# adaLN weight tiles spread over the four column groups of the tensor array, and put behind the score products of a head

## The chip, the cores and the metric

One Trainium2 chip, one core of it. The metric is the device time of one execution in microseconds (us), lower is better. Median before: 1648.79 us.

## What is computed

A two-layer hybrid backbone on 512 latent tokens behind 256 context tokens, 1024 channels, all in f32 accuracy. The part that the change touches is the adaLN modulation: for each layer, the two condition vectors (latent and context) go through silu and a product with a weight of 1024 x 3072, which gives shift, scale and gate.

```python
def layer(x, ctx, c, c_ctx, l):                       # core of the reference
    shift, scale, gate = split(silu(c) @ ada_w[l] + ada_b[l], 3)
    h = rms(x, norm_g[l]) * (1 + scale) + shift       # the same for ctx with c_ctx
    x = x + gate * mixer[l](h_ctx, h)                 # l = 0: HGRN2, 16 heads; l = 1: RG-LRU
```

## The kernel before, in words

**Staging.** All weights come from memory as tiles of 128 x 1024 f32 (512 KB) in one planned order (class Weights, DMA issue at L114 on SyncE's queue). A tile of the mixers is split by ScalarE (L129) and VectorE (L130) into two float32r parts, and each of their products is three matmuls (mm3, L308 to L310). Tiles of the adaLN weights (48: two layers, six blocks each, four tiles a block) are used as they come, in f32.

**An adaLN block** (ada_block, L223 to L249) makes 512 of the 3072 columns. The stationary operand is `sc`, silu of the two condition vectors padded to 32 columns, in eight chunks of 128 channels. It fills only 32 of the array's 128 columns, so the four tiles of a block go to four column groups (tile_position (0, 32j)), each with a part of the contraction:

```python
        for j in range(4):
            w = wget("ada", l, b, j)
            for k in range(2):
                PE.matmul(ps[32 * j:32 * j + 32, :], lhsT=sc[:, 2 * j + k, :], rhs=w[:, 512 * k:512 * k + 512],
                          start=k == 0, stop=k == 1, tile_position=(0, 32 * j))
            if j < 3:
                yield 480.0
```

So tile j is two matmuls of 512 columns, both in group j. An f32 matmul stands in the trace as two records (passes). Then ScalarE copies the block out of PSUM (blk, L233), four small matmuls add the four groups and turn the result (adat, L237), and VectorE adds the bias (L242, L246). Each yield ends a step: four steps with a tile, one with the transposes.

**Where the steps stand.** TensorE takes its work in program order. Blocks (0,0) to (0,3) are made in the start, in an order written by hand (START): a step "a0" is the next step of block (0,0), "r" the norm of the input (msh L259, rbh L269), "h3" chunk 3 of the modulated input, "f21" the part of the first head's product 2 with chunk 1. The blocks (0,4), (0,5) and (1,0) to (1,5) are made within heads 0, 1 and 9 to 14, one block a head. A head is a generator (hgrn): the diagonal scores (dg, L436), seven levels of scores (lv, L456), the states, the outputs. Scores of 32 keys use four column groups too: 24 matmuls of 32 columns. Between the steps of a head, interleave puts the products into the next head (in, L308 to L310), which are the filler. weave puts one step of the adaLN block after every third step of that filler.

Of the kernel before, what the change touches and what calls it, by code (L numbers as in the profile page):

```python
# [13 lines left out]
P = 128  # L14
CTX = 256
LAT = 512
NT = CTX + LAT          # tokens, context first
HN = NT // 2            # token half
ROWS, GW = 8, 64        # latent grid
DK = 8                  # 128-channel chunks of the model width  # L20
NH = 16                 # HGRN2 heads
NC = NT // P            # chunks of 128 tokens
NLEV = 7                # block sizes 1, 2, ... 64 within a chunk
NM = 5                  # of these, the ones within 32 tokens
RH = 8                  # RG-LRU heads
EPS = 1e-6

# the order of the start: a step of adaLN block b (ab), the norm (r), chunk k of h (hk), the weights of the first head's
# product y (wy), their part with chunk k of h (fky), the split of the first value weights (v)
# [3 lines left out]
# columns of the packed parameters  # L33
# [7 lines left out]
# columns of the constants: identity, row selector, 1/1024, 1/128  # L41
# [10 lines left out]
def perm(ap):  # L52
    """latent columns in column-major grid order, walked row by row"""
    return ap.rearrange("p (w r) -> p r w", r=ROWS)
# [6 lines left out]
def phase(main, weight, filler, total):  # L61
    """interleave up to the next None of main, if weight is that of one phase"""
    interleave(upto(main, weight), weight, filler, total)
# [12 lines left out]
class Nothing:  # L76
    """stands in for the program while the order of the weight tiles is taken down"""
# [16 lines left out]
class Weights:  # L94
    """the stream of [128, 1024] weight tiles, loaded ahead and split into two float32r parts"""
# [60 lines left out]
def interleave(main, weight, filler, total):  # L156
    """after each step of main (yields give its weight), its share of the filler (yields give its size)"""
    done, n = 0.0, 0.0
    for w in main:
        n += w  # L160
        while filler is not None and done < total * min(1.0, n / weight):
            try:
                done += next(filler)
            except StopIteration:
                filler = None
    run_all(filler)


def build(tc, ins, out, plan):
# [19 lines left out]
    # ---- constants, small parameters, the residual stream  # L189
# [24 lines left out]
    # silu of both condition vectors, padded to 32 columns  # L214
# [7 lines left out]
    # ---- adaLN: six blocks of 512 columns, four parts of the contraction side by side in the array  # L222
    def ada_block(l, b):  # L223
        ps = atile(f"ada{l}_{b}")
        for j in range(4):
            w = wget("ada", l, b, j)
            for k in range(2):
                PE.matmul(ps[32 * j:32 * j + 32, :], lhsT=sc[:, 2 * j + k, :], rhs=w[:, 512 * k:512 * k + 512],  # L228
                          start=k == 0, stop=k == 1, tile_position=(0, 32 * j))
            if j < 3:  # L230
                yield 480.0
# [19 lines left out]
    # ---- h = rms(x) * g * (1 + scale) + shift, as two float32r parts  # L251
    def rstd_of(accs, ones, tag, parts, between=()):
        """1 / sqrt(mean + eps) of each token from its squares (chunks of 128 tokens; the mean is over the partitions
        and accs), on all partitions: PSUM tiles of so many chunks"""
# [23 lines left out]
    def sumsq(accs, groups, tile_, k, c):  # L278
        """the squares of chunk k of the channels, summed by groups of chunks; the first of three groups on GpSimd"""
# [13 lines left out]
    def hchunk(l, k, i, rs, scr):  # L293
        """chunk k of h for one stretch of tokens; layer 0 keeps the latents in row-major order"""
# [9 lines left out]
    def mm3(ps, pairs, first=True, last=True, skip=False):  # L304
        """exact products of split operands: ps += sum over (whi, wlo, xhi, xlo) of whi xhi + whi xlo + wlo xhi"""
# [9 lines left out]
    # ================= layer 0  # L315
# [98 lines left out]
    def prep(h):  # L414
        """operands of the first two score steps"""
# [9 lines left out]
    def hgrn(h):  # L425
# [4 lines left out]
        # scores [key, query]: same token (both directions), then pairs of neighbouring blocks of 1, 2, ... 64 tokens;  # L430
        # up to 32 tokens the array works on four groups of 32 keys at once
# [9 lines left out]
        for l in range(NLEV):  # L441
# [5 lines left out]
            for c in range(NC):  # L447
                for g in range(P // w):
# [5 lines left out]
                    else:  # L454
                        rhs = QQ[:, 0, o - w:o]
                    PE.matmul(ps[w * g:w * g + w, w * c:w * c + w], lhsT=kt[:, o:o + w], rhs=rhs, start=c == 0,  # L456
                              stop=c == NC - 1, skip_group_check=True, tile_position=(0, w * g))
            kv = view(KK, 0, [[2 * B, n], [NT + B, 2], [1, B]])
# [22 lines left out]
        # keys with tokens on the partitions (in place), for the chunk states  # L481
# [7 lines left out]
        # states that enter the chunks, in the order of each direction  # L489
# [19 lines left out]
        # outputs, head norm, gate; latents written in column-major order of the grid  # L509
# [71 lines left out]
    # ---- start: norm of layer 0, the first head's q and forget gates as the chunks of h come  # L581
# [4 lines left out]
    # lower bound of layer 0: the first row of the softmax over the rows  # L586
# [44 lines left out]
    # layer 1: 8 softplus(-lam) = 8 (max(-lam, 0) + log1p(exp(-|lam|))), log1p as 2 atanh(y / (2 + y))  # L631
# [24 lines left out]
    # ---- heads: the products into the next head fill the tensor engine between the steps of this one  # L656
    def weave(gen, gens, every):
        """a step of gens after each so many of gen"""
        side = chain_(gens)
        for i, x in enumerate(gen):  # L660
            yield x
            if i % every == 0:
                next(side, None)
        run_all(side)

    def chain_(gens):
        for g in gens:
            yield from g
# [18 lines left out]
    for h in range(NH):  # L687
        if h == 0:
            fill, total = [v_item(0), in_item(0, 3), weave(head_in(1), extra(1), 3)], 54700.0
        elif h < NH - 1:  # L690
            fill, total = [weave(head_in(h + 1), extra(h + 1), 3)], 45300.0 if h < NH - 2 else 23500.0
        else:
            fill, total = [in_item(h, 3), out_item((h - 3, h - 2, h - 1))], 31400.0
        interleave(hgrn(h), HW, chain_(fill), total)
# [10 lines left out]
    # ================= layer 1: the context first  # L705
# [23 lines left out]
    def after(*names):  # L729
        """queue ScalarE's instructions behind the last ones of these kinds"""  # L730
# [14 lines left out]
    def conv(j, e, i, ps):  # L745
        """the centred convolution of one stretch of tokens; then the two parts of the result"""
# [39 lines left out]
    def mixer(j, groups):  # L786
        """gates of both directions, decay a, driven input u, scans; groups of directions and output chunks are taken in
        turn. ScalarE goes through its table sets once a group: sigmoid, exp and tanh, sqrt"""
# [4 lines left out]
        for keys in groups:  # L793
# [19 lines left out]
            # with T = tanh(-log(a)): 1 - a^2 = T (1 + a^2)  # L813
# [64 lines left out]
    # ---- the last head out, its first half ahead of the second; final norm  # L878
# [52 lines left out]
# ---- host: layouts only  # L931
def _layout(inp):
# [4 lines left out]
    chan = lambda v: v.reshape(-1, P).T                      # [n*128] -> [128, n]  # L937
    x = a["x"][0].reshape(ROWS, GW, 1024).transpose(1, 0, 2).reshape(LAT, 1024)
    xs = np.concatenate([a["ctx"][0], x], 0)                 # tokens x channels
# [24 lines left out]
    # adaLN columns: shift and scale chunks side by side, then the gates  # L964
# [4 lines left out]
    w = np.stack(blocks, 1)                                  # l, b, k, p, 512  # L969
    o["ada"] = w.reshape(2, 6, 4, 2, P, 512).transpose(0, 1, 2, 4, 3, 5).reshape(2, 6, 4, P, 1024)  # L970
# [31 lines left out]
```

## Time and profile before

| | |
|---|---|
| median of 3 runs | 1648.79 us (1645.66 to 1650.98) |
| span of the profiled execution | 1643.9 us |
| time of the profiled execution outside its span | not listed; the median is 4.9 us above the span |
| TensorE busy | 1595.2 us, 97% of the span |
| VectorE, ScalarE, GpSimd busy | 73%, 52%, 1% |
| mean DMA rate | 71 GB/s |
| adaLN products (L228) | 192 records, 81.2 us busy, 4% of the chain that ended last |

The chain that ended last is followed back from the last instruction. A busy TensorE counts as busy also when only one of its column groups works.

### The profile page before, as it was taken

The numbers are of one execution on the slowest core, as the hardware profiler recorded it, in microseconds if no ns is written. First come the engines' busy times: TensorE is split into PE (matmuls) and PEld (weight loads), VectorE is DVE, ScalarE is ACT, GpSimd is POOL, SyncE is SP. The second block draws the span as 40 slices with busy tenths as digits, with TensorE's granted clock in tenths as the row PEclk, the third lists the DMA queues.
The fourth block names the chain that finished last, engine by engine and source line by source line (L and its number), as shares of the span: only waits on it lengthen the run. The fifth ranks groups of instructions, "written<-read, shape, count | busy, mean of one in ns | idle before, by whom it ended". The sixth has DMA issues, their size and how long they took to land.

```text
span 1643.9 us, 33639 instructions
## 1 busy us (share of the span) xinstructions
PE 1595.2 (97%) x14548; PEld 1432.9 (87%) x14548; DVE 1203.1 (73%) x1867; ACT 856.0 (52%) x1359; POOL 11.8 (1%) x16
## 2 busy tenths in 40 slices
PE   6999999999999999999999999999999999999995
PEld 3888899999999999898989889888798888888884
DVE  5756668767867777756866675787758977887888
ACT  5544354444443453443444344544567677577774
POOL 0000000000000000000000000001000000000001
PEclk9999999999999999999999999999899999999997
DMA  8222211110211211213031222211022222222211
GB/s 340 65 78 65 91 53 47 58 53 27 75 43 40 66 53 40 82 61 97 33 117 48 82 78 65 89 42 40 26 91 76 74 68 77 74 68 64 78 64 51
DMA packets 33858, 116.76 MB, mean 71 GB/s; under 512 B 3632, under 2 KB 6064, under 8 KB 33712
## 3 DMA queue, kind: packets, MB, share of 16 engines
q1 hardware_dynamic: 32192, 113.26, 21.7%
q8 instruction: 114, 1.87, 0.5%
q10 hardware_dynamic: 1520, 1.37, 0.3%
q14 instruction: 32, 0.26, 0.0%
HBM read 112.52 MB, written 2.10 MB: 70 GB/s over the span
## 4 chain that ended last, share of the span: by engine, by line
PE 88%; DVE 7%; ACT 2%; issue 1%; DMA 1%; POOL 0%; ACTq 0%; POOLq 0%; DVEq 0%
PE in L308 12%; PE in L309 11%; PE in L310 11%; PE v L378 8%; PE ada L228 4%; PE lv L456 4%; PE o L531 3%; PE r L310 3%; PE r L308 3%; PE r L309 3%; PE o L308 3%; PE o L309 3%; PE o L310 2%; PE U L499 2%; PE gt L308 2%; PE gt L309 2%
## 5 line engine op out<-in xcount | busy, mean ns | idle before, releaser
L308 PE MATMUL in<-h_hi,hi 128*128 128x384 f32 x1024 | 355.1, 348 | 1.6 <-ACT h_hi L301 1.6
L309 PE MATMUL in<-h_lo,hi 128*128 128x384 f32 x1024 | 344.7, 337 | 0.4 <-DVE h_lo L302 0.4
L310 PE MATMUL in<-h_hi,lo 128*128 128x384 f32 x1024 | 344.4, 337 | 0.0
L129 ACT ACTIVATE hi<-raw 128x1024 fp32r<-128x1024 f32 x160 | 168.4, 1057 | 195.8 <-PE in L309 106.6
L130 DVE TENSOR_TENSOR lo<-raw,hi 128x1024 fp32r<-128x1024 f32 x160 | 195.0, 1220 | 92.9 <-ACT hi L129 92.8
L308 PEld LDWEIGHTS in<-h_hi,hi 128*128 128x128 f32 x1024 | 192.1, 188 | 35.9 <-issue 27.7
L309 PEld LDWEIGHTS in<-h_lo,hi 128*128 128x128 f32 x1024 | 192.6, 188 | 2.4 <-issue 1.7
L310 PEld LDWEIGHTS in<-h_hi,lo 128*128 128x128 f32 x1024 | 192.3, 188 | 1.7 <-DVE amul L246 0.8
L466 DVE TENSOR_TENSOR QQ<-QQ,T 128x768 f32<-128x768 f32 x112 | 117.4, 1048 | 94.1 <-PE lv L456 94.1
L412 ACT ACTIVATE kt<-KK 128x768 f32<-128x768 f32 x112 | 102.1, 912 | 52.9 <-DVE KK L459 50.0
L310 PE MATMUL r<-h_hi,lo 128*128 128x512 f32 (+1 forms) x344 | 123.7, 360 | 3.7 <-DVE lo L130 3.7
L334 ACT ACTIVATE sg<-in 128x384 f32<-128x384 f32 x128 | 61.9, 485 | 125.2 <-PE in L310 125.1
L459 DVE TENSOR_TENSOR KK<-KK,T 128x768 f32<-128x768 f32 x112 | 117.0, 1045 | 11.7 <-ACT kt L412 11.7
L309 PE MATMUL r<-h_lo,hi 128*128 128x512 f32 (+1 forms) x344 | 123.1, 358 | 0.0
L308 PE MATMUL r<-h_hi,hi 128*128 128x512 f32 (+1 forms) x344 | 123.0, 358 | 0.0
L378 PE MATMUL v<-hi,h_hi 128*128 128x256 f32 x384 | 111.9, 291 | 0.0
L378 PE MATMUL v<-lo,h_hi 128*128 128x256 f32 x384 | 107.5, 280 | 0.0
L378 PE MATMUL v<-hi,h_lo 128*128 128x256 f32 x384 | 107.4, 280 | 0.0
L228 PE MATMUL ada<-raw,sc 128*32 128x512 f32 x192 | 81.2, 604 | 14.2 <-DMA raw<-in_ada_dram 14.2
L554 DVE RECIPROCAL sq<-sq 128x384 f32<-128x384 f32 x30 | 75.9, 2541 | 21.3 <-ACT sq L548 21.2
L402 DVE SCALAR_TENSOR_TENSOR x<-o,ada,x 128x256 f32<-128x256 f32 (+1 forms) x184 | 82.2, 490 | 12.6 <-PE o L310 12.2
L308 PE MATMUL o<-rhi,hi 128*128 128x384 f32 (+2 forms) x240 | 86.2, 361 | 2.2 <-DVE lo L130 1.2
(202 smaller groups left out, 3286.2 us busy)
## 6 DMA issues: line engine op xcount, KB each, us to landing
raw<-in_hgw_dram SPq DMA_DIRECT2D x64, 512.0 KB, 3.5
raw<-in_ada_dram SPq DMA_DIRECT2D x48, 512.0 KB, 3.7
raw<-in_rgi_dram SPq DMA_DIRECT2D x32, 512.0 KB, 3.8
raw<-in_hgv_dram SPq DMA_DIRECT2D x16, 512.0 KB, 3.4
raw<-in_hgo_dram SPq DMA_DIRECT2D x16, 512.0 KB, 3.5
raw<-in_rgg_dram SPq DMA_DIRECT2D x16, 512.0 KB, 3.5
raw<-in_rgo_dram SPq DMA_DIRECT2D x16, 512.0 KB, 3.8
x<-in_x_dram SPq DMA_DIRECT2D x8, 384.0 KB, 6.0
```

The lines of the kernel that those rows point to most:

```text
L129: self.nc.scalar.activation(hi, r, AF.Copy)
L130: self.nc.vector.tensor_tensor(lo, r, hi.bitcast(F32), ALU.subtract)
L228: PE.matmul(ps[32 * j:32 * j + 32, :], lhsT=sc[:, 2 * j + k, :], rhs=w[:, 512 * k:512 * k + 512], start=k == 0, stop=k == 1, tile_position ...
L308: PE.matmul(ps, lhsT=wh, rhs=xh, start=first and i == 0, stop=False, skip_group_check=skip)
L309: PE.matmul(ps, lhsT=wh, rhs=xl, start=False, stop=False, skip_group_check=skip)
L310: PE.matmul(ps, lhsT=wl, rhs=xh, start=False, stop=last and i == n - 1, skip_group_check=skip)
L378: PE.matmul(ps, lhsT=xh[:, kk, t], rhs=w[:, k], start=part == 0 and k == 0 and i == 0 and c % 2 == 0, stop=part == 1 and k == 3 and i == 2 ...
L402: V.scalar_tensor_tensor(xs, ps[:, a - c.start:b - c.start], gate[:, d, 1 - j:2 - j], xs, ALU.mult, ALU.add)
L412: A.activation(view(kt, 0, [[2 * B, n], [B, 2], [1, B]]), view(KK, 0, [[2 * B, n], [NT + B, 2], [1, B]]), AF.Copy)
L459: V.tensor_tensor(kv, kv, view(T, 1, [[2, n], [m - 1, 2], [0, B]]), ALU.mult)
L466: V.tensor_tensor(qv, qv, view(T, m + 1, [[2, n], [-m - 1, 2], [0, B]]), ALU.mult)
L554: V.reciprocal(rs, rs)
```

## The change

Three edits, all of them about the adaLN blocks. (1) A tile now holds 256 of the block's columns for four chunks of the contraction, and its four matmuls of 256 columns go to the four column groups, one each. Two tiles make one half of the columns. The host's layout of the weights follows. (2) In the heads, weave is gone: hgrn takes the adaLN steps as `side` and takes one right behind the score products of each level. (3) START itself is the same. Comments were taken out too, so line numbers shift (L228 becomes L230, L237 L240, L308 to L310 L311 to L313, L456 L460, L436 L440).

```diff
         for j in range(4):
             w = wget("ada", l, b, j)
-            for k in range(2):
-                PE.matmul(ps[32 * j:32 * j + 32, :], lhsT=sc[:, 2 * j + k, :], rhs=w[:, 512 * k:512 * k + 512],
-                          start=k == 0, stop=k == 1, tile_position=(0, 32 * j))
+            half, part = divmod(j, 2)
+            for g in range(4):
+                PE.matmul(ps[32 * g:32 * g + 32, 256 * half:256 * half + 256], lhsT=sc[:, 4 * part + g, :],
+                          rhs=w[:, 256 * g:256 * g + 256], start=j == 0, stop=j == 3, skip_group_check=True,
+                          tile_position=(0, 32 * g))
             if j < 3:
                 yield 480.0
...
-    def hgrn(h):
+    def hgrn(h, side):
...
                     PE.matmul(ps[w * g:w * g + w, w * c:w * c + w], lhsT=kt[:, o:o + w], rhs=rhs, start=c == 0,
                               stop=c == NC - 1, skip_group_check=True, tile_position=(0, w * g))
+            next(side, None)
             kv = view(KK, 0, [[2 * B, n], [NT + B, 2], [1, B]])
...
-    def weave(gen, gens, every):
-        side = chain_(gens)
-        for i, x in enumerate(gen):
-            yield x
-            if i % every == 0:
-                next(side, None)
-        run_all(side)
...
         if h == 0:
-            fill, total = [v_item(0), in_item(0, 3), weave(head_in(1), extra(1), 3)], 54700.0
+            fill, total = [v_item(0), in_item(0, 3), head_in(1)], 54700.0
         elif h < NH - 1:
-            fill, total = [weave(head_in(h + 1), extra(h + 1), 3)], 45300.0 if h < NH - 2 else 23500.0
+            fill, total = [head_in(h + 1)], 45300.0 if h < NH - 2 else 23500.0
         else:
             fill, total = [in_item(h, 3), out_item((h - 3, h - 2, h - 1))], 31400.0
-        interleave(hgrn(h), HW, chain_(fill), total)
+        side = chain_(extra(h + 1) if h < NH - 1 else [])
+        interleave(hgrn(h, side), HW, chain_(fill), total)
+        run_all(side)
...
-    w = np.stack(blocks, 1)
-    o["ada"] = w.reshape(2, 6, 4, 2, P, 512).transpose(0, 1, 2, 4, 3, 5).reshape(2, 6, 4, P, 1024)
+    w = np.stack(blocks, 1)
+    w = w.reshape(2, 6, 2, 4, P, 2, 256)
+    o["ada"] = w.transpose(0, 1, 5, 2, 4, 3, 6).reshape(2, 6, 4, P, 1024)
```

What moves on TensorE is seen best in the order of its instructions. A row is line, operation, output<-inputs (buffer numbers behind the names), the tile's shape and how many alike follow each other.

**The start.** The first rows of TensorE before (raw0 to raw3 are the tiles of block (0,0), raw5 and raw7 the first two of block (0,1)):

```order
L228 MATMUL ada0_0_179<-raw0_180,sc_99 32x512 x2
L259 MATMUL msh0_200<-cst_78,acc0_143 128x1 x6
L228 MATMUL ada0_0_179<-raw1_182,sc_99 32x512 x2
L228 MATMUL ada0_0_179<-raw2_184,sc_99 32x512 x2
L228 MATMUL ada0_0_179<-raw3_186,sc_99 32x512 x2
L269 MATMUL rbh0_0_218<-cst_78,rh0_207 128x128 x2
L269 MATMUL rbh0_2_221<-cst_78,rh0_207 128x128 x4
L237 MATMUL adat0_0_234<-cst_78,blk0_0_232 128x2 x4
L228 MATMUL ada0_1_250<-raw5_190,sc_99 32x512 x2
L228 MATMUL ada0_1_250<-raw7_194,sc_99 32x512 x2
```

and of the change:

```order
L230 MATMUL ada0_0_179<-raw0_180,sc_99 32x256 x4
L262 MATMUL msh0_202<-cst_78,acc0_143 128x1 x6
L230 MATMUL ada0_0_179<-raw1_182,sc_99 32x256 x4
L230 MATMUL ada0_0_179<-raw2_184,sc_99 32x256 x4
L272 MATMUL rbh0_0_224<-cst_78,rh0_209 128x128 x2
L272 MATMUL rbh0_2_227<-cst_78,rh0_209 128x128 x4
L230 MATMUL ada0_0_179<-raw3_186,sc_99 32x256 x4
L240 MATMUL adat0_0_242<-cst_78,blk0_0_240 128x2 x4
L230 MATMUL ada0_1_258<-raw5_190,sc_99 32x256 x4
L311 MATMUL in0_0_0_256<-h_hi_94,hi4_250 128x384
```

The fourth tile of block (0,0) now stands behind the products rbh, and the second tile of block (0,1) no longer stands beside the first. Of the 16 tiles of the start, two now stand directly beside each other (raw1, raw2) and three more at the end of block (0,3); before, there were such runs of 3, 2, 2 and 3.

**A head.** TensorE within head 9, third tile of block (1,0), before:

```order
L309 MATMUL in10_1_1_7789<-h_lo_95,hi85_7718 128x384
L310 MATMUL in10_1_1_7789<-h_hi_94,lo85_7719 128x384
L228 MATMUL ada1_0_7636<-raw86_7716,sc_99 32x512 x2
L308 MATMUL in10_1_1_7789<-h_hi_94,hi85_7718 128x384
L309 MATMUL in10_1_1_7789<-h_lo_95,hi85_7718 128x384
```

and of the change:

```order
L312 MATMUL in10_1_0_7780<-h_lo_95,hi85_7761 128x384
L313 MATMUL in10_1_0_7780<-h_hi_94,lo85_7762 128x384
L460 MATMUL lv9_2_7809<-QQ9_7278,kt9_2_7770 32x32 x24
L230 MATMUL ada1_0_7677<-raw86_7759,sc_99 32x256 x4
L311 MATMUL in10_1_1_7847<-h_hi_94,hi85_7761 128x384
```

The tile stood alone between products of the whole array and now follows the scores of level 2. This holds for all 32 tiles of the heads: before, 22 stood right behind scores and 10 alone; now each block has its tiles behind levels 0, 1, 2 and 3, and its transposes behind level 4.

**The end of head 14.** TensorE where the last block's last tile stood before (pm are the sums of the head's norm, in15 the products into head 15):

```order
L531 MATMUL o14_1_11978<-QQ14_11145,S14_11907 128x128 x2
L546 MATMUL pm14_0_11992<-shi14_11958,ones_r_90 128x384
L547 MATMUL pm14_0_11992<-slo14_11959,ones_r_90 128x384
L228 MATMUL ada1_5_11577<-raw138_11865,sc_99 32x512 x2
L308 MATMUL in15_2_1_12017<-h_hi_94,hi137_11867 128x384
L309 MATMUL in15_2_1_12017<-h_lo_95,hi137_11867 128x384
```

and where head 15 begins, before:

```order
L309 MATMUL o12_0_0_12270<-rlo12_10543,hi140_12095 128x384
L310 MATMUL o12_0_0_12270<-rhi12_10542,lo140_12096 128x384
L308 MATMUL o12_0_0_12270<-rhi13_11322,hi141_12254 128x384
L436 MATMUL dg15_12067<-q15_11531,kd15_12052 32x32 x24
L456 MATMUL lv15_0_12113<-QQ15_12051,kt15_0_12053 32x32 x24
```

and of the change:

```order
L312 MATMUL in15_3_1_12256<-h_lo_95,hi139_12033 128x384
L313 MATMUL in15_3_1_12256<-h_hi_94,lo139_12034 128x384
L311 MATMUL in15_3_1_12256<-h_hi_94,hi139_12033 128x384
L440 MATMUL dg15_12163<-q15_11619,kd15_12155 32x32 x24
L460 MATMUL lv15_0_12209<-QQ15_12154,kt15_0_12156 32x32 x24
```

Between head 14's norm and head 15's first scores there is no adaLN tile any more, and the scores of head 15 stand 17 products earlier, within the products in15_3_1 instead of behind them.

## Rows read from the trace of the kernel before

**Rows 1.** The page: engines (part 1), chain (part 4), the adaLN group (part 5).
```profile
PE 1595.2 (97%) x14548; PEld 1432.9 (87%) x14548; DVE 1203.1 (73%) x1867; ACT 856.0 (52%) x1359; POOL 11.8 (1%) x16
...
PE 88%; DVE 7%; ACT 2%; issue 1%; DMA 1%; POOL 0%; ACTq 0%; POOLq 0%; DVEq 0%
...
L228 PE MATMUL ada<-raw,sc 128*32 128x512 f32 x192 | 81.2, 604 | 14.2 <-DMA raw<-in_ada_dram 14.2
```

**Rows 2.** Busy time of PE, PEld, DVE, ACT, POOL by stretch, PEclk, DMA share, GB/s.
```profile
10.00:15.00 5.00, 0.79 (x1) 0.18 (x2) 4.41 (x10) 4.97 (x8) 0.00 (x0) 1.00 1.03 411
...
609.50:673.70 64.20, 64.20 (x715) 61.78 (x714) 50.96 (x88) 28.77 (x49) 0.00 (x0) 1.00 0.13 42
673.70:746.00 72.30, 72.30 (x787) 64.06 (x786) 46.33 (x73) 31.76 (x56) 0.00 (x0) 1.00 0.24 74
```

**Rows 3.** Weight loads in a tile of head 0: start, us, instruction [idle before].
```profile
102.37 0.11 PEld L228 LDWEIGHTS ada<-raw,sc 128*32 128x32 f32 x1 [0.32 <-issue]
102.80 0.11 PEld L228 LDWEIGHTS ada<-raw,sc 128*32 128x32 f32 x1 [0.32 <-issue]
```

**Rows 4.** PE timeline of head 9: level without tile, tile alone, level with tile.
```profile
691.99 0.63 PE L456 MATMUL lv<-QQ,kt 128*32 128x32 f32 x48
692.54 0.44 PE L308 MATMUL in<-h_hi,hi 128*128 128x384 f32 x1
...
694.40 0.34 PE L309 MATMUL in<-h_lo,hi 128*128 128x384 f32 x1
694.57 0.34 PE L310 MATMUL in<-h_hi,lo 128*128 128x384 f32 x1
694.84 1.90 PE L228 MATMUL ada<-raw,sc 128*32 128x512 f32 x4
696.67 0.44 PE L308 MATMUL in<-h_hi,hi 128*128 128x384 f32 x1
...
703.91 0.63 PE L456 MATMUL lv<-QQ,kt 128*32 128x32 f32 x48
704.38 1.88 PE L228 MATMUL ada<-raw,sc 128*32 128x512 f32 x4
706.19 0.45 PE L308 MATMUL in<-h_hi,hi 128*128 128x384 f32 x1
```

**Rows 5.** PE timeline: level 0 of head 9, and one pass of a level by itself.
```profile
676.56 0.72 PE L456 MATMUL lv<-QQ,kt 128*32 128x32 f32 x48
677.09 1.89 PE L228 MATMUL ada<-raw,sc 128*32 128x512 f32 x4
...
1048.85 0.20 PE L456 MATMUL lv<-QQ,kt 128*32 128x32 f32 x1
```

**Rows 6.** PE and DVE timelines of the start up to the first product into head 0.
```profile
14.21 3.30 PE L228 MATMUL ada<-raw,sc 128*32 128x512 f32 x4 [14.21 <-DMA raw<-in_ada_dram]
17.44 1.50 PE L259 MATMUL msh<-cst,acc 128*128 128x1 f32 x12
18.87 1.93 PE L228 MATMUL ada<-raw,sc 128*32 128x512 f32 x12
20.73 1.60 PE L269 MATMUL rbh<-cst,rh 128*128 128x128 f32 x12
...
26.62 0.97 PE L308 MATMUL in<-h_hi,hi 128*128 128x384 f32 x4 [1.65 <-ACT h_hi L301]
...
12.27 4.15 DVE L286 TENSOR_TENSOR acc<-acc,sq 128x768 f32<-128x768 f32 x4
```

**Rows 7.** PE groups of 27.9 to 57 us: adaLN tiles among head 0's products.
```profile
L228 PE MATMUL ada<-raw,sc 128*32 128x512 f32 x40 | 13.6, 599 | 0.0
```

**Rows 8.** PE and DVE timelines around the passage from head 14 to head 15.
```profile
1096.52 0.64 PE L456 MATMUL lv<-QQ,kt 128*32 128x32 f32 x48 [0.65 <-DVE QQ L466]
...
1082.63 0.16 DVE L242 TENSOR_TENSOR ada<-adat,prm 128x4 f32<-128x4 f32 x1 [1.68 <-PE adat L237]
...
1086.46 2.55 DVE L554 RECIPROCAL sq<-sq 128x384 f32<-128x384 f32 x1
```

## The prediction

> **What bounds the kernel now.** I read the page first. TensorE is busy for 97% of the span and the chain that ended last is 88% TensorE; the adaLN products have 192 records and 81.2 us of busy time [rows 1]. That busy time is no price, since records of different column groups lie beside each other in it. So the second view is the busy time by stretch, around two neighbouring heads: one without an adaLN block takes 64.20 us, the next, with a block, 72.30, and in both TensorE has no idle time (64.20 of 64.20, 72.30 of 72.30), while VectorE, the next, is busy 50.96 and 46.33 [rows 2]. A block in a head therefore costs 72.30 - 64.20 = 8.1 us, all of it on the path that sets the end. The third view is TensorE's timeline, for what one tile costs where it stands [rows 4], and the fourth the start, where tiles stand among waits [rows 6, 7].
>
> **What a tile costs.** Two weight loads of one tile follow each other by 102.80 - 102.37 = 0.43 us [rows 3]: that is one pass of 512 columns. A tile before has four, all in one column group, one behind the other: 1.72 us. The timeline agrees. From level scores with a tile behind them to the next product it is 706.19 - 703.91 = 2.28 us, without a tile 692.54 - 691.99 = 0.55 [rows 4], so such a tile costs 1.73. A tile alone stands between two products that start 696.67 - 694.57 = 2.10 apart [rows 4], where neighbours start 694.57 - 694.40 = 0.17 apart; that is 1.93, and the product behind it has its next neighbour 0.1 later than usual (0.44 long instead of 0.34), so 2.03. The 0.3 more is what going into 32-column products and back costs; behind scores it is paid already.
>
> The changed tile has eight passes of 256 columns, two in each of the four groups. I take 0.215 for such a pass, half of 0.43. If the four groups run side by side, the tile takes 2 x 0.215 = **0.43 us**. The trace before has no tile of this form, so the bounds come from the nearest rows. Below: 0.43, as no row shows a pass faster than 0.43 for 512 columns. Above: eight passes in a row, 1.72. I take the lower end, by two rows. Three tiles that stand beside each other in the start, twelve passes in three groups, take 1.93 instead of 3 x 1.72 [rows 6], so three streams run at full rate beside each other. And scores put 48 passes of 32 columns on four groups, interleaved as the new tile is: at 0.43 x 32/512 = 0.027 each a single file would be 1.29 us, and the row is 0.63 long with 0.55 to the next product [rows 4].
>
> A rule speaks against this, and the row is first: in program order those twelve passes are four of one group, four of the next, four of the third, and yet they take hardly more than the four of one tile (1.93 against 1.90) [rows 4, 6]. The Trainium skill, page "TensorE: Matmul & The Clock Gate", Part 3, section "The mechanism", says that matmuls start and end strictly in program order and only weight loads are pulled ahead. By it the twelve passes could overlap only at the seams between groups, which the trace does not bear out; by it the new tile would be the third rival below, and the sum some 20 us in place of 50.
>
> **The sum, part by part.**
>
> Heads: of the 32 tiles, 22 stand behind scores and 10 alone before, 22 x 1.73 + 10 x 2.03 = 58.4 us. Afterwards all 32 stand behind scores (the order shows it), each 0.43 + 0.01 as measured against 1.72: 32 x 0.44 = 14.1. Gain 44.3.
>
> Passage from head 14 to head 15: there a tile alone (2.03) and the transposes (8.1 - 3 x 1.73 - 2.03 = 0.9) go, 2.9 us of work. They covered VectorE's chain of the head's norm (a reciprocal of 2.55, and the first levels of head 15 already wait 0.65 for QQ [rows 8]). VectorE itself gets rid of a 1.68 wait for the transposes there [rows 8], and 17 products now follow the first scores in place of preceding them and fill part of the hole. Of the 2.9 between 0 and all is lost again; with 1.68 of VectorE's chain shortened the loss is some 1.2 to 1.6: 1.4. Heads together 42.9.
>
> Start, up to the first product into head 0: the first tile needs two rounds in place of four, so the norm's sums msh no longer wait for it but for acc, ready at 12.27 + 4.15 = 16.42 instead of 17.44 [rows 6]: 1.0 earlier. Between msh and rbh two tiles (0.86 + 0.1) replace three (20.73 - 18.87 = 1.86 [rows 6]), and the third follows rbh alone (0.43 + 0.1): 0.3 earlier. First product 1.3 earlier. There is an odd row here: the first tile's passes took 3.30 / 4 = 0.82, twice the usual, while the granted clock of the stretch reads 1.00 [rows 2, 6]. If that lasts over the next two tiles, 0.9 of the 1.3 is gone.
>
> Start, behind it: 40 records, that is ten tiles, stand in eight stretches from 28.49 on; they are busy for 13.6 us [rows 7]. By price it is 28 passes in a row, 12.0, plus 8 x 0.32 for going in and out, 14.6. Afterwards eleven tiles stand here in nine stretches: 11 x 0.43 + 9 x 0.32 = 7.6. The START order lost its neighbours' overlap, but a tile alone is now as short as a quarter of one. Gain 7.0. Against this the chunks of the modulated input come from VectorE and ScalarE; TensorE waits 1.65 for them at the first product [rows 6], and pushed 8 us closer to them it will wait more: I take 1.0 (0 to all 8.3). Start together 1.3 + 7.0 - 1.0 = 7.3.
>
> At nothing: bytes and weight loads of DMA are the same, at a share of 0.13 to 0.24 in the heads [rows 2]; only the start is full (1.03 in 10 to 15 [rows 2]), and it is among the bounds of the start. Two more passes per product load their weights under passes that run. In the heads the tiles now come evenly, four levels in a row, each 0.44 ahead of the next product; VectorE and ScalarE have 26 and 40 us free in such a head [rows 2], so the level's own chain has room. If it had not, the wait would show at the scores as in head 15.
>
> Sum: 42.9 + 7.3 = 50.2. The profiled span of 1643.9 becomes 1593.7; the median of the runs shown is 4.9 above the span, and I keep that: 1648.8 - 50.2 = **1598.6 us**.
>
> **The rivals.**
> - *The start gives its gain back*: chunks of the input or tiles in flight (DMA share 1.03) hold TensorE as long as before. For it the 1.65 wait [rows 6]; against it that from 28.49 on TensorE has tiles and products without a wait. Time 1598.6 + 7.3 = 1606.
> - *Four streams at once are slower than three.* For it: level 0 of a head, with its scattered reads, is 0.72 long, one pass of it 0.20 [rows 5], so twelve rounds take 0.52, 43 ns each, against the 27 of the full rate. At 43/27 a tile is 0.69, 0.26 more, over 32 + 15 stretches' tiles 12 us: 1611.
> - *Matmuls start in program order only.* Passes come group by group, so the second pass of a group holds up the next group's first: five rounds of 0.215, 1.07 a tile, 0.64 x 47 = 30 us more: 1629. Against it the twelve passes in 1.93 [rows 6].
> - *Slower than before*: the four groups of one tile do not overlap at all, say because all four read the same weight tile. The tile is then 1.72 as before. In the heads only 10 x 0.3 for going in and out stays, less 1.4: 1.6 gained. In the start the overlap of neighbours is lost: 11 x 1.72 + 9 x 0.32 = 21.8 for 14.6, and 3.6 more around rbh: 10.8 lost. Time 1648.8 + 9.2 = 1658. The change turns to a loss from 0.43 + 50.2 / 47 = 1.50 us a tile. Against it the 48 passes of scores in 0.63 [rows 4], which read their keys from one tile too.
> - *It does not do what it says*: the order shows that it does; what is left is that the tiles were somehow free, against the 8.1 per head [rows 2]. No change.
>
> **How the numbers follow.** Forecast 0.68, start given back 0.12, slower streams 0.10, program order 0.05, no overlap 0.03, nothing 0.02. The forecast's own range is 1594 (no loss at the passage or in the start, 1596.2, less 2 for the spread of the runs) to 1606. The range given, 1594 to 1613, takes in the first two rivals and leaves out the others and the forecast's tails, under 2 in 10. A measurement of this kernel can tell some 0.3%, 5 us, from no change. Faster 0.95, same 0.02, slower 0.03.
>
> **What would show it.** Right: the adaLN group with 384 records; from a level's scores to the next product about 0.55 + 0.44 = 1.0 us in heads 9 to 13, with no idle TensorE; head 9 at 64.2 + 4 x 0.44 + 0.9 = 66.9 us; the first product into head 0 near 25.3; a wait for VectorE at the first levels of head 15. Wrong: a tile of 0.7 (slower streams), 1.07 (program order) or 1.7 (no overlap) behind the scores; or waits for h_hi and h_lo in the start that add up to several us.

## The result, and the profile after

The changed kernel takes **1604.51 us** (four runs, 1603.88 to 1605.08) beside 1649.78 us before (four runs, 1645.66 to 1650.98): ratio 0.9733, 95% interval 0.9718 to 0.9749. That is 45.3 us less; 50.2 less and 1598.6 us were forecast, with a range of 1594 to 1613. Faster, as forecast, and inside the range, but the parts of the sum came out unevenly. The page of the changed kernel, engines and chain:

```profile
PE 1549.6 (97%) x14740; PEld 1430.2 (89%) x14740; DVE 1203.0 (75%) x1867; ACT 856.5 (53%) x1359; POOL 11.8 (1%) x16
...
PE 85%; DVE 9%; ACT 3%; issue 1%; DMA 0%; POOL 0%; POOLq 0%; DVEq 0%; ACTq 0%
```

Against [rows 1], TensorE lost 45.6 us of busy time and still sets the end; nothing else moved. There are 384 adaLN records now, which the view of their line shows with the least, the median and the longest duration in ns:

```profile
L230 PE MATMUL ada<-raw,sc x384: 378/385/636, 14.0 to 1010.2; 128*32 128x256 f32 x192
```

**The heads.** The same two stretches as [rows 2], a head without a block and head 9 with one (columns as there):

```profile
598.18:662.37 64.19, 64.19 (x715) 61.79 (x714) 50.94 (x88) 28.77 (x49) 0.00 (x0) 1.00 0.14 43
662.37:729.27 66.90, 66.90 (x803) 63.19 (x802) 46.41 (x73) 31.74 (x56) 0.00 (x0) 1.00 0.26 80
```

Head 9 takes 66.90 us, the number that was forecast, and TensorE has no idle time in it: a block costs 2.7 us in place of 8.1. TensorE's timeline of that head shows one level with a tile and the level with the transposes:

```profile
665.23 0.72 PE L460 MATMUL lv<-QQ,kt 128*32 128x32 f32 x48
665.75 0.63 PE L230 MATMUL ada<-raw,sc 128*32 128x256 f32 x8
666.31 0.44 PE L311 MATMUL in<-h_hi,hi 128*128 128x384 f32 x1
...
678.12 0.60 PE L460 MATMUL lv<-QQ,kt 128*32 128x32 f32 x46
...
679.11 0.44 PE L311 MATMUL in<-h_hi,hi 128*128 128x384 f32 x1
...
688.83 0.63 PE L460 MATMUL lv<-QQ,kt 128*32 128x32 f32 x48
689.39 1.05 PE L240 MATMUL adat<-cst,blk 128*128 128x2 f32 x8
690.31 0.42 PE L311 MATMUL in<-h_hi,hi 128*128 128x384 f32 x1
```

From scores to the next product it is 679.11 - 678.12 = 0.99 us with a tile, where [rows 4] has 0.55 without and 2.28 with an old one: the new tile costs 0.44, as priced.

**The start** is another matter. Its timeline on TensorE, to be laid beside [rows 6]:

```profile
14.04 1.08 PE L230 MATMUL ada<-raw,sc 128*32 128x256 f32 x8 [14.04 <-DMA raw<-in_ada_dram]
16.51 2.72 PE L262 MATMUL msh<-cst,acc 128*128 128x1 f32 x12 [1.39 <-DVE acc L289]
19.16 1.93 PE L230 MATMUL ada<-raw,sc 128*32 128x256 f32 x16
21.02 2.93 PE L272 MATMUL rbh<-cst,rh 128*128 128x128 f32 x12
23.88 0.87 PE L230 MATMUL ada<-raw,sc 128*32 128x256 f32 x8
...
26.46 0.64 PE L230 MATMUL ada<-raw,sc 128*32 128x256 f32 x8
29.56 1.01 PE L311 MATMUL in<-h_hi,hi 128*128 128x384 f32 x2 [2.46 <-ACT h_hi L304]
```

msh does start 0.9 us earlier than before, as forecast. But it takes 2.72 us where it took 1.50, rbh 2.93 where it took 1.60, and two tiles 1.93, as long as three old ones. Of these tiles only the one at 26.46 takes 0.64. TensorE works at half its rate, 1.2 of 2.4 GHz by these durations, up to about 24 us: the trace's first record of the clock stands at 24.4, with the full rate (before: at 17.1, in the first tile). In the wait for the first product the granted clock falls to half again, from 27.8 to 34.6 (columns as in [rows 2]):

```profile
27.80:34.60 6.80, 4.73 (x18) 2.98 (x19) 6.68 (x9) 4.27 (x5) 0.00 (x0) 0.50 0.36 110
```

The first product into head 0 comes at 29.56, three us later than before, and head 0's first scores (dg) at 74.96 instead of 76.38. Of these 1.4 us, 1.0 is only a change of order: eight of the products v, 0.12 us each, stood ahead of the scores before and stand behind them now. A mark with the same work ahead of it in both kernels is the first product v, before and then after the change:

```profile
69.69 0.29 PE L378 MATMUL v<-hi,h_hi 128*128 128x256 f32 x1
```

```profile
69.22 0.29 PE L381 MATMUL v<-hi,h_hi 128*128 128x256 f32 x1
```

Where the profiled span went from 1643.9 to 1603.3, by this mark and by the first start of the sums msv:

| stage | before | after | gain |
|---|---|---|---|
| start, up to head 0's first product v | 69.69 | 69.22 | 0.5 (forecast 7.3) |
| heads, from there to the sums msv in head 15 | 1056.87 | 1014.21 | 42.7 (forecast 42.9) |
| msv to the end | 517.4 | 519.9 | -2.5 (forecast 0) |

The spans differ by 40.6 only, the medians by 45.3: the profiled execution of before is one of its short ones. The experiments show part of why both kernels scatter.

### The profile page after: what moved, and what is told of

Same layout as the page of the kernel before. It is cut to its first block, busy times and chain, and to the rows that moved or that the text cites. A ratio compares the mean times of both kernels' runs of the same rounds, so it can differ in the third digit from the quotient of the medians.

```text
span 1603.3 us, 33990 instructions
## 1 busy us (share of the span) xinstructions
PE 1549.6 (97%) x14740; PEld 1430.2 (89%) x14740; DVE 1203.0 (75%) x1867; ACT 856.5 (53%) x1359; POOL 11.8 (1%) x16
## 4 chain that ended last, share of the span: by engine, by line
PE 85%; DVE 9%; ACT 3%; issue 1%; DMA 0%; POOL 0%; POOLq 0%; DVEq 0%; ACTq 0%
PE in L311 12%; PE in L312 11%; PE in L313 11%; PE v L381 8%; PE lv L460 4%; PE o L536 4%; PE r L313 3%; PE r L311 3%; PE r L312 3%; PE o L311 3%; PE o L312 3%; PE o L313 3%; PE U L504 2%; PE gt L311 2%; PE gt L312 2%; PE gt L313 2%
## 5 line engine op out<-in xcount | busy, mean ns | idle before, releaser
L311 PE MATMUL in<-h_hi,hi 128*128 128x384 f32 x1024 | 354.8, 348 | 3.4 <-ACT h_hi L304 2.7
L313 PE MATMUL in<-h_hi,lo 128*128 128x384 f32 x1024 | 345.0, 337 | 0.0
L311 PEld LDWEIGHTS in<-h_hi,hi 128*128 128x128 f32 x1024 | 192.7, 188 | 20.2 <-issue 8.6
L313 PEld LDWEIGHTS in<-h_hi,lo 128*128 128x128 f32 x1024 | 192.7, 188 | 0.9 <-issue 0.4
L313 PE MATMUL r<-h_hi,lo 128*128 128x512 f32 (+1 forms) x344 | 123.8, 360 | 3.7 <-DVE lo L130 3.7
L311 PE MATMUL r<-h_hi,hi 128*128 128x512 f32 (+1 forms) x344 | 123.0, 358 | 0.0
L311 PE MATMUL o<-rhi,hi 128*128 128x384 f32 (+2 forms) x240 | 87.0, 364 | 2.2 <-DVE lo L130 1.2
L460 PEld LDWEIGHTS lv<-QQ,kt 128*32 128x32 f32 (+1 forms) x4992 | 63.4, 113 | 28.6 <-issue 20.8
```

The lines of the kernel that those rows point to most:

```text
L311: PE.matmul(ps, lhsT=wh, rhs=xh, start=first and i == 0, stop=False, skip_group_check=skip)
L313: PE.matmul(ps, lhsT=wl, rhs=xh, start=False, stop=last and i == n - 1, skip_group_check=skip)
```

## The experiments

Theory **clock**: the new tiles are as cheap in the start as in the heads, but with less work there TensorE stays at half its rate and gives the gain back. Rival **inputs**: the modulated input, from VectorE and ScalarE, sets the start at any rate. And for the heads: is it the tile's form or its place that pays, and does the fullest column group set a tile's time? Each group of four kernels ran beside the same runs of the kernel before (1648.18 for e1 to e4, 1646.82 for e5 to e8, 1647.78 for e9 to e12).

**e1, a busy start.** Products that nobody reads, in time in which TensorE waited:

```diff
+    def idle_work(name, n):
+        t = dtile(name)
+        for _ in range(n):
+            PE.matmul(t[:, :256], lhsT=ident, rhs=x1[:, 0, :256], start=True, stop=True)
...
         if what == "a":
+            if step == 0:
+                idle_work("idle0", 12)
             next(blocks[n[0]])
+            if step == 0:
+                with tc.issue_after(getattr(mark[0], "ins", mark[0])):
+                    idle_work("idle1", 4)
```

> The changed kernel with TensorE kept busy in the start by products that nobody reads: 12 (24 passes of 256 columns) before the first adaLN tile and 4 between it and the sums msh. They sit in time where TensorE only waits. Theory clock (the start's gain of 7 us was lost because the shorter tiles left TensorE at half its rate from 14 to 26 and from 29 to 35 us): msh takes about 1.5 us as before the change, not 2.72, rbh 1.6, not 2.93, the first product into head 0 comes near 25.5 instead of 29.56, head 0's first scores near 70 instead of 74.96, time about 1599 to 1600. Theory inputs (the chunks of the modulated input, from VectorE and ScalarE, set the start whatever TensorE's rate): first scores not before 74, time 1603 to 1605.

Measured: **1597.77 us**, 50.4 below before (ratio 0.9701, 0.9687 to 0.9716). TensorE's timeline of e1:

```profile
6.30 6.84 PE L611 MATMUL idle<-x,cst 128*128 128x256 f32 x24 [6.30 <-DMA cst<-in_cst_dram]
13.78 0.64 PE L232 MATMUL ada<-raw,sc 128*32 128x256 f32 x8 [0.65 <-DMA raw<-in_ada_dram]
14.35 1.99 PE L611 MATMUL idle<-x,cst 128*128 128x256 f32 x8
16.34 1.50 PE L264 MATMUL msh<-cst,acc 128*128 128x1 f32 x12
17.77 1.50 PE L232 MATMUL ada<-raw,sc 128*32 128x256 f32 x24
19.20 1.60 PE L274 MATMUL rbh<-cst,rh 128*128 128x128 f32 x12
...
25.03 0.97 PE L313 MATMUL in<-h_hi,hi 128*128 128x384 f32 x4 [1.77 <-ACT h_hi L306]
```

msh, tiles and rbh run at the full rate, the first product comes at 25.03 (25.3 was the price-based forecast), the first scores at 68.19, 6.8 us earlier than in the changed kernel. The clock theory gave 25.5, 70 and 1599 to 1600; inputs gave 74 or later. Inputs falls. Two things limit this. e1's order also differs: three tiles stand between msh and rbh in place of two, and adat no longer waits 0.72 for blk; msh is slow in the changed kernel before the two orders part, but how much of the 6.8 is order no run separates. And behind its own wait of 1.77 e1 too loses the rate for 3.4 us:

```profile
26.20:29.60 3.40, 3.25 (x14) 2.00 (x15) 2.69 (x4) 0.35 (x1) 0.00 (x0) 0.51 0.90 360
```

e10, the same kernel in another group, has 68.14 and 1596.36 us:

> e1 once more, unaltered, beside e9, e11 and e12. Theory clock: first scores of head 0 at 68 to 68.5 again, 50 us below before.

**e7, the same in the kernel before** (12 products ahead of the first tile, 2 behind it).

> The kernel before with the busy start of e1 (12 products before the first adaLN tile, 2 behind it). Theory clock with the prices of the prediction: at the full rate on both sides the new tiles are worth 1.3 + 7.0 us in the start, so the first scores of head 0 come 7 to 8 us behind e1's 68.2, near 75 to 76, hardly earlier than the 76.4 without the products; time 1645 to 1648. Theory that the added products help any start by 6 us: first scores near 70, time about 1641.

Measured: first scores at 75.52, 1646.44 us (ratio 0.9991, 0.9981 to 1.0001). The added products do next to nothing for the old tiles. By the first product v, 68.82 here against 62.45 in e1, the new tiles are worth 6.4 us in a start with these products (1.0 of the 7.3 between the first scores is again the eight products v). The first product into head 0 comes 26.58 - 25.03 = 1.55 earlier, where 1.3 was priced; behind it 4.8 are gained, where 7.0 were priced. e7 keeps the full rate from 12.3 us on through the start, so e1's 3.4 us at half rate are lost from that; an estimate from its 3.25 busy us there is 1.6. The prices of the forecast hold roughly; the changed kernel could not collect them.

**e6, the change once more**, unaltered.

> The changed kernel once more, unaltered. If the half rate in the start belongs to the order of its work, the first scores of head 0 come at 74.5 to 75.5 again and the first product into head 0 near 29.5; if it is chance, at 68 to 70. Time 1603 to 1606.

Measured: first product at 29.67, first scores at 75.37, msh 2.72 and rbh 2.93 us long; 1601.41 us, 45.4 below its own runs of before. So the half rate is not the accident of one execution: msh takes 2.72 us in all five profiles that start with the new tiles and have nothing behind the first (the change, e3, e6, e8, e11). Nor does the order of work alone decide it. e4, told below, has the start of the kernel before, old tiles in the same order up to the first product v, without a hole between first tile and msh:

```profile
14.05 3.59 PE L229 MATMUL ada<-raw,sc 128*32 128x512 f32 x4 [14.05 <-DMA raw<-in_ada_dram]
17.58 2.72 PE L260 MATMUL msh<-cst,acc 128*128 128x1 f32 x12
20.23 3.65 PE L229 MATMUL ada<-raw,sc 128*32 128x512 f32 x12
23.80 2.36 PE L270 MATMUL rbh<-cst,rh 128*128 128x128 f32 x12
```

Here msh and the tiles go at half rate too, the first record of the full rate stands at 25.4, where before and e2 (the same old tiles) have it at 17.1, and the first product v comes at 73.03 in place of 69.69. With the rate down on both sides the new tiles (69.22 in the change, 69.63 in e6) are 3.4 to 3.8 us ahead. What made the rate rise early in two executions of this start and late in the third is not shown.

**e11 and e12, which of the two helps.** e11 keeps the 12 products ahead of the first tile only, e12 the 4 behind it only.

> e1 with only the 12 products ahead of the first adaLN tile. After the tile TensorE waits about 2 us for acc, then come products of one column. If TensorE's rate falls back in that hole: msh 2.7 and rbh 2.9 us again, first scores near 74. If the work before is enough: msh 1.5, first scores 68 to 69.

> e1 with only the 4 products between the first adaLN tile and msh. At half rate they take 3.4 us and hold msh up to about 18.4, two us later than in the changed kernel; but TensorE is then busy from 14 to 18 as it was before the change. If that work is what raises its rate: msh 1.5, rbh 1.6, first scores near 70. If the gap from 15 to 16.5 had nothing to do with it: msh 2.7, rbh 2.9, first scores near 77.

e11: first scores at 75.74, 1601.96 us. Its timeline, and the granted clock of two stretches (the last but two column):

```profile
13.84 0.64 PE L232 MATMUL ada<-raw,sc 128*32 128x256 f32 x8 [0.35 <-DMA raw<-in_ada_dram]
16.53 2.72 PE L264 MATMUL msh<-cst,acc 128*128 128x1 f32 x12 [2.05 <-DVE acc L291]
19.18 1.93 PE L232 MATMUL ada<-raw,sc 128*32 128x256 f32 x16
21.05 2.69 PE L274 MATMUL rbh<-cst,rh 128*128 128x128 f32 x12
...
29.11 1.01 PE L313 MATMUL in<-h_hi,hi 128*128 128x384 f32 x2 [2.46 <-ACT h_hi L306]
```

```profile
14.00:20.00 6.00, 3.95 (x28) 3.03 (x24) 2.46 (x4) 1.72 (x3) 0.00 (x0) 0.71 1.03 413
20.00:26.00 6.00, 5.28 (x40) 3.82 (x32) 0.00 (x0) 2.52 (x4) 0.00 (x0) 0.72 1.02 408
```

The first tile runs at the full rate (0.64), then TensorE waits 2.05 us for acc, and msh is at half rate again: with the hole open, 7 us of work ahead of it did not keep the rate. The granted clock shows it here, 0.71 in 14 to 20 (its records have half from 16.5 to 23.3); e10, with the hole filled, has 1.00 there. In the changed kernel that column says 1.00 in the same stretches although the durations are doubled: the trace has no record of the clock before 24.4, and the column reads 1.00 where there is none. In the first microseconds the durations are the better witness. e12: the four products took 3.78 us, msh came 2.0 us late at 18.55, and from there through rbh the work went at or near the full rate; behind the wait of 2.45 before the first product it fell to half again, from 26.3 to 33.1:

```profile
14.97 3.78 PE L611 MATMUL idle<-x,cst 128*128 128x256 f32 x8
18.55 1.85 PE L264 MATMUL msh<-cst,acc 128*128 128x1 f32 x12
...
21.76 1.60 PE L274 MATMUL rbh<-cst,rh 128*128 128x128 f32 x12
```

First scores at 71.04, 1600.31 us. So two us of delay bought back four. In the profile of before, the long old tile stood in the same place, at 14.21 to 17.44 [rows 6], and the rate rose in it; in e4 the same tile did not bring it up.

**e2, old tiles in the start, new ones in the heads.**

```diff
+            if l == 0 and b < 4:
+                for k in range(2):
+                    PE.matmul(ps[32 * j:32 * j + 32, :], lhsT=sc[:, 2 * j + k, :], rhs=w[:, 512 * k:512 * k + 512],
+                              start=k == 0, stop=k == 1, tile_position=(0, 32 * j))
+            else:
...
+    w[0, :4] = first[0, :4]
```

> The changed kernel, but blocks (0,0) to (0,3) in the old form of tile with the old layout of their weights; heads as changed. If the start gained only 1.4 us by the new tiles, as the first scores of head 0 say (76.38 to 74.96): first scores at 76.4, time about 1606. If the new tiles' 7 us are in the time elsewhere: about 1611.

Measured: first product at 26.35, first product v at 69.42 beside 69.22 in the change, first scores at 75.16, 1604.73 us (ratio 0.9738, 0.9724 to 0.9753, beside 0.9733 of the change). In the start the change as it stands is worth nothing that these runs can tell.

**e3, the form alone; e4, the place alone.** e3 is the kernel before with the new tile and layout and the old weave; e4 has hgrn(h, side) with the old tile and layout.

> The kernel before with the new form of tile and its layout alone; steps woven in after every third filler step, so 22 tiles of the heads behind scores, 10 alone. By the price of going in and out (0.3 a tile alone) 3.0 us more than the changed kernel, less what the passage from head 14 to 15 lost there (about 1): 1606 to 1608. If the places carried the gain: near 1645.

> The kernel before with the new places alone (one step right behind the scores of each level), tiles in the old form. By the price of 0.3 us for each of 10 tiles that stood alone 3.0 us less than before, less about 1 at the passage from head 14 to 15: 2 us faster, so 1644 to 1648. If the place were what counts: near 1610.

Measured: e3 **1602.89 us** (ratio 0.9735, 0.9721 to 0.975), e4 **1646.84 us** (0.999, 0.9979 to 1.0001). The gain is the form's. Since the start scatters, the place is better read from head 0's first product v to msv: 1056.87 us before, 1053.87 in e4 (3.0 less, where 2.0 was expected), 1016.15 in e3 against 1014.21 in the change (1.9 less; a block costs 67.20 - 64.19 = 3.0 us in e3, 2.7 in the change). e3 came out below the 1606 to 1608 expected for it, which started from the change's 1604.5; behind msv its profile has 515.6 us, that of the change 519.9. e5 comes to this stretch.

**e8, two groups instead of four** in the second and fourth tile of a block:

```diff
-                PE.matmul(ps[32 * g:32 * g + 32, 256 * half:256 * half + 256], lhsT=sc[:, 4 * part + g, :],
+                p = g if part == 0 else g % 2
+                PE.matmul(ps[32 * p:32 * p + 32, 256 * half:256 * half + 256], lhsT=sc[:, 4 * part + g, :],
                           rhs=w[:, 256 * g:256 * g + 256], start=j == 0, stop=j == 3, skip_group_check=True,
-                          tile_position=(0, 32 * g))
+                          tile_position=(0, 32 * p))
```

> The changed kernel with the second and fourth tile of each block on two column groups (two matmuls each) in place of four; the sums over groups stay right. If the fullest group sets the time: such a tile takes 4 x 0.215 = 0.86 us, so 0.86 more a block in the heads, heads 9 to 13 at 67.7 to 67.8 instead of 66.9, 6.9 us more in all heads and up to 3.4 in the start: 1611 to 1614. If all eight passes of a tile share one stream, or start in program order only: heads 9 to 13 stay within 0.2 of 66.9.

Measured: 1612.07 us (ratio 0.9789, 0.9772 to 0.9806), 10.7 above e6, the change in the same group. Head 9:

```profile
666.01:733.73 67.72, 67.72 (x804) 63.65 (x803) 46.45 (x73) 31.75 (x56) 0.00 (x0) 1.00 0.25 79
```

67.72 - 66.90 = 0.82 us more for two such tiles (0.76 against e6's head 9, 66.96), where 0.86 was expected: the fullest column group sets the time of a tile, at about 0.2 us a pass of 256 columns. The records of single passes agree: in head 9 a tile on two groups starts its passes in four pairs, 0.22 us apart (676.81, 677.03, 677.24, 677.46). This settles the prediction's rivals on TensorE. Shared or slower streams, and matmuls that start in program order only, would not make the same eight passes longer by just the two that moved to each of two groups. The Trainium skill, page "TensorE: Matmul & The Clock Gate", Part 3, section "The mechanism", has matmuls start and end strictly in program order; for passes in different column groups the runs here disagree, with 0.44 us for a tile that this rule would put at 1.07. In the three old tiles side by side of [rows 6] the first passes start at 18.87, 18.88 and 18.90, one of each tile, although in program order each tile's four passes stand together.

**e5, busy also at the layer boundary and at the end.** e1, and 10, 9 and 9 products more in three later waits.

> The busy start of e1, and products that nobody reads in three more waits: 10 (20 passes of 128 columns, some 2.1 us) before the last head's outputs, 9 between them and the second sums msh of layer 1's norm, 9 before the last sums msf of the final norm. Theory clock: the stretch from the last msv to the first rc is no longer 25 to 27 us but 23 or less, the first rc to the first r 28.4 or less, from the first msf to the end 15.4 or less in place of 16.6; time about 1591 to 1594, and the runs lie closer together than the 3 to 5 us of the other kernels. Theory chance or inputs: time as e1, 1597 to 1599, or longer by the added 6 us.

Measured: 1599.98 us (ratio 0.9711, 0.9694 to 0.9729), no better than e1, and the expectation missed: msv to rc 29.9 us, rc to r 29.8, msf to the end 16.9. TensorE's timeline at the boundary:

```profile
1095.29 0.61 PE L264 MATMUL msh<-cst,acc 128*128 128x1 f32 x4 [1.83 <-POOL acc L291]
...
1102.55 2.17 PE L323 MATMUL idle<-cst 128*128 128x128 f32 x18
1104.56 1.05 PE L264 MATMUL msh<-cst,acc 128*128 128x1 f32 x8
1107.17 0.39 PE L313 MATMUL rc<-h_hi,hi 128*128 128x256 f32 x1 [1.56 <-ACT h_hi L306]
```

TensorE has the full rate from 29.2 to 1107.8 here, and the sums msh wait 1.83 us for GpSimd's acc. My expectations gave this stretch as 25 to 27 us, counted from the wrong mark; from the first msv to the first rc it is 29.6 us in ten of the fourteen profiles (before, e2, e3, e6 to e12, to 0.1), 29.9 in e5, 31.9 in the changed kernel, 33.6 in e1 and e4. In the changed kernel the granted clock falls to half there:

```profile
1097.00:1101.00 4.00, 4.00 (x17) 3.68 (x17) 4.00 (x9) 2.54 (x7) 2.62 (x3) 0.50 0.54 167
1101.00:1105.00 4.00, 4.00 (x12) 3.01 (x11) 2.35 (x5) 1.22 (x3) 0.37 (x1) 0.50 0.21 84
```

e6, the same program, had 29.6. So the 2.5 us that the change seems to lose behind msv are chance of one execution. That 29.6 is a bound by other engines is argued from e5, which had the full rate and no less time; no run isolates it. Like the tail (msf to the end 15.4 or 16.6), the stretch is part of the scatter of all these kernels.

**e9, constants later.** The softplus constants of layer 1 move from ahead of head 0 into head 3.

> The busy start of e1, and the softplus constants of layer 1 (lines spt, needed only there) worked out in head 3 instead of ahead of head 0. In the changed kernel TensorE waits 0.96 us for them at level 1 of head 0, and head 0 gained 4.5 us where by the prices it should gain 6.1 (four tiles at 0.44 for one at 1.73 and three at 2.03). If that wait is the reason: head 0 takes 70.2 instead of 71.2 us, and the time is 1.0 us below e10. If VectorE's chain of the level is late anyway: 71.2 again.

The waits of TensorE in head 0, the changed kernel and then e9:

```profile
PE lv L460 <- DVE spt L650: 1.0, 1, 1.0
```

```profile
PE lv L462 <- DVE QQ L473: 0.4, 1, 0.4
```

Measured: 1596.84 us beside 1596.36 of e10. Head 0 itself takes 69.12 us, but its first scores come at 69.87 in place of 68.14, since eleven products v more stand ahead of them. By the common mark, from the first product v to the scores of head 1, e9 takes 76.22 us and e10 77.01: 0.8 of the 0.96 came back. In the time nothing shows: e9's first product v came 0.4 later than e10's, and at head 13 nothing is left of the lead. The expected 1.0 in the time did not come.

## Why the prediction was right where it was, and where not

- **What a tile costs**: right, in size and mechanism. 0.44 us behind scores, head 9 at 66.90 us. The lower bound was taken for two rows of before (three tiles side by side, scores in 0.63), and e8 shows that the reason was the right one.
- **Heads, gain 44.3 less 1.4**: 42.7 measured from the first product v, where two misses of 0.6 to 0.7, at both ends, cancel. Heads 9 to 13 gained 5.4 us each, as priced. Head 0 gained 5.4 from that mark to the scores of head 1 (82.36 to 76.93) where 6.1 was its share; the wait of 0.96 for VectorE's constants at level 1 covers the difference (e9 got 0.8 of it back). So "the level's own chain has room" failed there, for work of VectorE that is not the level's. At the passage from head 14 to head 15, 86.72 us from head 14's scores to msv against 91.34 before is a gain of 4.6, 0.8 less than another block's 5.4, where 1.4 less was taken. The wait that was to show the loss did not grow: for QQ TensorE waits 0.7 us there in place of 1.3, and the longest wait is a new one for r:

```profile
1052.22 0.44 PE L311 MATMUL o<-r,hi 128*128 128x384 f32 x1 [1.12 <-ACT r L574]
```

- **Start, 1.3 + 7.0 - 1.0**: the failed step. 0.5 measured. The prices were roughly right (6.4 with the busy start, e7 against e1), the rate was not. I had the row of the first tile, 0.82 us a pass at a granted clock of 1.00, called it odd, put at most 0.9 on it and left that out of the sum. What it shows is that TensorE starts at half its rate; in that execution the rate rose while this tile ran. The change shortens the tile to 1.1 us and leaves a hole of 1.4 behind it; the rate stays down to 24.4 us, falls again in the wait of 2.46 for the first product and comes back at 34.6. The profile that I forecast from also had a good start: with the same work e4 had the full rate only at 25.4. The sign of being wrong that I gave, waits for h_hi and h_lo of several us, came in part: 3.0 us in place of 2.0, and behind a late msh and rbh.
- **The rival "the start gives its gain back"**, with 0.12, is what happened, for a cause that it did not name: at 1606 it is nearer than the forecast to 1604.5, and the waits that it meant (chunks, tiles in flight) are not what set the start (e1). The time lies in the range because the range was drawn to take in this rival; that the start came out there for another reason is luck.
- **The other rivals** are out: slower streams, program order and no overlap by head 9's 66.90 and by e8; "does not do what it says" by all of it.
- **From span to time**: I kept the 4.9 us between span and median. A run of the change took 1605.08 us with a span of 1603.3, 1.8 more; the rest of the 4.9 is that the profiled execution of before was a short one.

## What to carry to other kernels

For a product that fills a quarter of the array's columns, cutting it so that every weight tile feeds all four column groups at once paid here: its time was the passes of the fullest group, and neighbours were no longer needed for an overlap. Before shortening work at the head of a kernel, look at TensorE's rate there: where a stretch shows passes of twice the usual length, prices taken at the full rate may not hold in the next one, and one profile does not tell when the rate rises. To compare stages of two kernels, take a mark with the same work ahead of it in both. Filling a hole with products that nobody reads brought 5 to 7 us here in the start of the changed kernel (e1, e10), nothing in that of the old one (e7), and nothing at the layer boundary and the end (e5).

The fastest kernels of the study are e10 and e1, the change with a busy start: ratio to before 0.9686 (0.9672 to 0.9701) and 0.9701 (0.9687 to 0.9716), beside 0.9733 (0.9718 to 0.9749) of the change. e9, at 0.9685, is not told apart from them.

## What the hardware showed that I had not expected

- After 7 us of products and a tile at the full rate, a hole of 2.05 us was followed by half rate from 16.5 to 23.3 us (e11); with the hole filled, e1 and e10 kept the full rate to 26.2 and 25.6 and lost it for 3.4 us behind a wait of 1.7 to 1.8 for the first product.
- The same work in the same order had the full rate at 17.1 us in one execution (before) and at 25.4 in another (e4), 3.3 us apart at the first product v.
- Products of one column cost time by the rate too: msh, twelve passes, runs 1.40 to 1.50 us at the full rate and 2.72 at half, though it streams twelve columns in all.
- What one execution has of the rate at the layer boundary is worth up to 4 us from msv to rc (29.6 to 33.6) with the program unaltered (e1 33.6, e10 29.6).
